# adaLN tiles of the FFNs in buffers of their own, requested two steps before they are reduced

## The chip, the cores and the metric

One core of a Trainium2 chip runs the whole program. The metric is the device time of one execution in microseconds, the median of several runs. The core has five engines that run side by side and meet only at semaphores: TensorE (PE), VectorE (DVE), ScalarE (ACT), GpSimd (POOL) and SyncE (SP). Here SP does nothing but request DMA transfers from HBM, in the order of its program; DVE, ACT and PE too work through their instructions strictly in order, so that one that waits holds up all that stand behind it on its engine.

## What is computed

Two layers, each of three sub-layers: FFN, token mixer, FFN. Every sub-layer is modulated by a conditioning vector c (adaLN) and followed by a residual sum and a LayerNorm:

```python
mod = (silu(c) @ ada_w[l] + ada_b[l]).reshape(-1, 3, 3, 1024)   # shift, scale, gate of three sub-layers
g, up = split(u @ w_in);   F(u) = (silu(g) * up) @ w_out        # FFN, D_FF = 2816
h = 0.5 * F(x * (1 + scale) + shift)
x = LayerNorm(ALPHA * x + (1 + gate) * h)
```

There are 256 tokens, so x fits on chip; what comes from HBM is the weights, each used once. The adaLN weights are part of them: each of the 18 vectors of 1024 numbers (shift, scale, gate of six sub-layers) is a 1024x1024 matrix times silu(c).

## The kernel before

**Products.** Every product of the network is done as three matmuls of numbers split in a high and a low part (`split_mm`, L286 to L288 with the weights stationary, L290 to L292 with the activations stationary): high by high, low by high, high by low. A weight tile of 128x1024 (512 KB) comes into a buffer named `raw` (L259), ACT casts its high part `hi` (L262), DVE subtracts to get the low part `lo` (L267), and then PE can use it.

**The buffers.** The tag `raw` has five such buffers. A request on SP waits until the buffer it will overwrite has been read for the last time, for a weight by the subtraction L267.

**The FFN.** There are 22 blocks f of 128 hidden columns. The first two of all but the first FFN are done for token half t = 0, then t = 1, with the tokens stationary (tiles `acc`, `th`, `h`; the transposes back to hidden columns, `hT`, are L609). From then on a block is one `hidden(f)`: 48 matmuls into a PSUM bank `mm`, tanh on ACT (`th`, L522), two DVE operations (`th` L523 and `h` L525, the last readers of the bank), a cast on ACT (`hh`, L531) and a subtraction on DVE (`hl`, L532). The down products (`acc<-hi,hh` and so on) follow a few blocks later. In PSUM the banks rotate, so PE cannot begin a block until the h of an earlier one has been made.

**The boundary.** At the end of a sub-layer `boundary` makes the residual sum and the statistics (L401 to L408) of token half 0 and then 1, normalises (L418), and PE transposes the result (L426), from which the next `uh` and `ul` are made (L432 to L437). The scale and shift of the LayerNorm are applied to x itself later (L485, L486). PE fills the time with down products and with the first blocks of the next FFN.

**adaLN.** The vectors of the next sub-layer and the gate of the current one are made beside this. `ada_cols` gives four steps to a vector; each step requests two tiles of 128x1024 on SP (L307) and reduces each of them on DVE (L308, multiply by silu(c) and sum along the row). An FFN has twelve such steps, 24 tiles, spread over the blocks f (the last one, with nothing behind it, four); a mixer has twelve. The 128 reductions of the program therefore use the same five `raw` buffers as the weights, and a step's request stands next to its reduction in the program.

**Order.** The order on each engine is fixed before the run, by a scheduler that takes instructions by priority and by modelled readiness. `behind()` keeps the first steps of a sub-layer from being placed before the boundary's main work.

**Other buffers.** The tag `big8` has three buffers of 8 KB a partition. It holds tiles of the mixers (`mh`, `ml`, `merged`, the live row tiles), the start's `xT` and `ada0`, and `rt` of each boundary. In an FFN's blocks they are not used until `rt` is (L629).

Of the kernel before, what the change touches and what calls it, by code (L numbers as in the profile page):

```python
# [11 lines left out]
F32 = mybir.dt.float32  # L12
# [44 lines left out]
RB, QB = 5, 15  # L57
# [6 lines left out]
GD = 3  # L64
# [39 lines left out]
SS = 1  # L104
PJ = 5
AFF = 3
AM = 42
ROW_M = 10

# [35 lines left out]
def trunk(ctx: ExitStack, tc: tile.TileContext, x, xT, crow, ada0, adac, adab, w_in0, w_in0x, gcol, bcol, ln_g, ln_b,  # L145
          w_in, w_out, mpair, mv0, mv12, mbrA, mbr, mwo, bgate, bforget, eye, rot, masks, out):
    nc = tc.nc
    P = 128
    cp = ctx.enter_context(tc.tile_pool(name="cp", bufs=1))
    wp = ctx.enter_context(tc.tile_pool(name="wp", bufs=3))  # L150
    ap_ = ctx.enter_context(tc.tile_pool(name="ap", bufs=2))
    sp = ctx.enter_context(tc.tile_pool(name="sp", bufs=2))
    mp = ctx.enter_context(tc.tile_pool(name="mp", bufs=1))
# [140 lines left out]

    mods = {(l, s): {} for l in range(DEPTH) for s in range(3)}

    def ada_cols(l, s, v):

        key = ("shift", "scale", "gate")[v]

        def run(c):
            if c == 0:
                mods[(l, s)][key] = ap_.tile([P, KT], F32, tag=key, bufs=2, name=key)
            t = mods[(l, s)][key]
            for n in (2 * c, 2 * c + 1):
                raw = wp.tile([P, 1024], F32, tag="raw", bufs=RB, name="raw")
                nc.sync.dma_start(raw, adac[l, s, v, n])  # L307
                nc.vector.tensor_tensor_reduce(raw, raw, cond_row, 0.5, adab_sb[:, l * 3 + s, v, n:n + 1],  # L308
                                               ALU.mult, ALU.add, accum_out=t[:, n:n + 1])

        return [lambda c=c: run(c) for c in range(4)]

    def ada_gate(l, s):

        def spread():
            ps = tp_bank()
            nc.tensor.transpose(ps[:KT, :P], mods[(l, s)]["gate"], ident)
            col = ap_.tile([KT, P], F32, tag="grow8", bufs=1, name="grow8")
            nc.scalar.copy(col, ps[:KT, :P])
            flat = dp.tile([KT, P], F32, tag="gflat", bufs=2, name="gflat")  # L320
            nc.gpsimd.dma_start(flat, col)
            G = ap_.tile([P, D], F32, tag="row", bufs=3, name="G")
            fetch_row(G, flat.rearrange("a b -> (a b)"))
            mods[(l, s)]["G"] = G

        return spread
# [18 lines left out]
    def fetch_row(dst, row):  # L345

        with tc.issue_after(held["pool"]):
            nc.gpsimd.memset(dst, 0.0)
        nc.gpsimd.dma_start(dst[0:P:32], row.partition_broadcast(4))

    def spread_row(dst):
        for h in range(SH):
            hs = slice(h * (D // SH), (h + 1) * (D // SH))
            with tc.issue_after(held["lo"]):
                nc.vector.stream_shuffle(dst[:, hs], dst[:, hs], [0] * 32)

    def both(*fs):
        def run():
            for f in fs:
                f()  # L360
        return run

    def sub_steps(l, s, nxt):

        st = mods[(l, s)]
        nx = ada_cols(*nxt, 0) + ada_cols(*nxt, 1) if nxt else [lambda: None for _ in range(8)]

        def fetch(key, row):
            st[key] = ap_.tile([P, D], F32, tag="row", bufs=3, name=key)
            fetch_row(st[key], row)  # L370

        before = {}
        for key, n, src in (("g", ROW_M if s == 1 else ROW_G, ln_g), ("b", ROW_M if s == 1 else ROW_B, ln_b)):
            before.setdefault(n, []).append(lambda key=key, src=src: fetch(key, src[l * 3 + s]))
            before.setdefault(n + GD, []).append(lambda key=key: spread_row(st[key]))
        before.setdefault(GG, []).append(lambda: ada_gate(l, s)())
        before.setdefault(GG + GD, []).append(lambda: spread_row(st["G"]))
        seq = ada_cols(l, s, 2) + nx + ([lambda: None] * (ROW_M + GD + 1 - 12) if s == 1 else [])
        return [both(*before.get(n, []), f) for n, f in enumerate(seq)]


# [112 lines left out]
    def ffn(l, s, u, nxt, steps, first=False):  # L494
# [12 lines left out]
        def hidden(f):  # L507
            k0 = N0 if f in part else 0
            w = load(w_in[fi, f, :, k0:].rearrange("p a b -> p (a b)"))
            ps = mm_bank()  # L510
            for g in range(2):
                for kt in range(k0, KT):
                    split_mm(ps[:, g * 256:(g + 1) * 256], w((kt - k0) * 256 + g * 128, 128),
                             uh[:, kt, :], ul[:, kt, :], kt == k0, kt == KT - 1)
            if f in part:
                nc.vector.tensor_tensor(part[f], part[f], ps, op=ALU.add)
                ps = part[f]
            post(f, ps[:, :256], ps[:, 256:])
# [93 lines left out]
        for f in range(f0, NF):  # L612
            hidden(f)
            if not first and f >= AFF and held["affine"]:
                held["affine"].pop(0)()
# [23 lines left out]
    def mixer(l, u, nxt, steps):  # L639
# [12 lines left out]
        def on(n, *fs):  # L652
            turns.setdefault(n, []).extend(fs)
# [323 lines left out]
        def plan():  # L977
# [27 lines left out]
            for n, piece in enumerate(held["affine"]):  # L1005
                on(AM + n, piece)

# [114 lines left out]
    for l in range(DEPTH):  # L1122
        u = ffn(l, 0, u, (l, 1), sub_steps(l, 0, (l, 1)), first=l == 0)
        u = mixer(l, u, (l, 2), sub_steps(l, 1, (l, 2)))
        nxt = (l + 1, 0) if l + 1 < DEPTH else None
        u = ffn(l, 2, u, nxt, sub_steps(l, 2, nxt))
# [55 lines left out]
```

## Time and profile before

| what | value |
|---|---|
| time, median of 3 runs | 1320.27 us (1318.94 to 1322.92) |
| the profiled execution's own time | 1320.82 us |
| its span on the engines | 1319.0 us |
| PE busy | 1271.0 us, 96% |
| DVE busy | 1036.8 us, 79% |
| ACT busy | 653.7 us, 50% |
| moved by SP's queue | 298 MB, 66.5% of the 16 DMA engines |

The sub-layers lie at about 0 to 205 us (FFN), 205 to 455 (mixer), 455 to 655 (FFN), 655 to 850 (FFN of the second layer), 850 to 1100 (mixer) and 1100 to 1319 (FFN). The table's shares are means over all of them. In the list of waits a row names the engine and tile that sat idle, what it waited for, and how long in total, how often and how long at most; in a timeline a row is one instruction or a run of equal ones, with the idle time before it in brackets. Start-to-start, matmuls of 256 columns follow one another at about 0.12 us and those of 512 at 0.23 us, though each shows a longer time of its own, since they overlap.

### The profile page before, as it was taken

Reading aid. Unit: us, or ns where it says so; the run is one execution under the profiler, and the core shown is the slowest. Engines: PE = TensorE matmul, PEld = TensorE weight load, DVE = VectorE, ACT = ScalarE, POOL = GpSimd, SP = SyncE. Lnnn points to the kernel's source line nnn. Section 1 sums busy time; section 2 is a strip of 40 time slices with the busy share of each in tenths; the row PEclk is TensorE's granted clock in tenths of the full one; section 3 lists DMA queues with packets and bytes.
Section 4 is the critical chain, followed back from the end, with each engine's and each line's share of the span. In section 5 each row is a group of like instructions: output and inputs, shape, how many; then the busy total and the mean of one; then the engine's idle time right before and its main releaser. Section 6 shows DMA issues by size and latency. Waiting matters only on the chain.

```text
span 1319.0 us, 23422 instructions
## 1 busy us (share of the span) xinstructions
PE 1271.0 (96%) x9178; PEld 1180.2 (89%) x9178; DVE 1036.8 (79%) x1701; ACT 653.7 (50%) x1023; POOL 134.2 (10%) x150
## 2 busy tenths in 40 slices
PE   6999999999999999999999999999999999999997
PEld 5989988899899889999989999898989998899995
DVE  7788888999765799876698877698976758976565
ACT  4555355456664454444355444445657544554440
POOL 0130000304111000000000000022050110000000
PEclk9999999999999999999999999999999999999999
DMA  9889893767665638987449887356676554595540
GB/s 340 327 290 330 294 306 133 243 191 245 228 216 180 215 128 312 309 279 262 159 166 320 289 296 237 115 178 219 217 235 233 192 192 160 208 317 193 185 137 32
DMA packets 85846, 300.41 MB, mean 228 GB/s; under 512 B 10604, under 2 KB 12316, under 8 KB 85736
## 3 DMA queue, kind: packets, MB, share of 16 engines
q1 hardware_dynamic: 84392, 298.00, 66.5%
q8 instruction: 72, 1.18, 0.4%
q10 hardware_dynamic: 576, 0.60, 0.1%
q0 software_dynamic: 768, 0.32, 0.1%
q14 instruction: 38, 0.31, 0.1%
HBM read 297.81 MB, written 1.07 MB: 227 GB/s over the span
## 4 chain that ended last, share of the span: by engine, by line
PE 41%; issue 26%; DVE 13%; DMA 12%; ACT 4%; POOL 3%; DVEq 0%; ACTq 0%; SPq 0%; POOLq 0%
PE mm L286 8%; PE mm L287 8%; PE mm L288 8%; DMA raw<-in_w_in_dram 7%; DVE lo L267 5%; PE acc L292 3%; PE acc L290 3%; PE acc L291 3%; ACT hi L262 2%; POOL lb L968 2%; DVE raw L308 2%; DMA raw<-in_adac_dram 1%; PE tp L286 1%; PE tp L287 1%; PE tp L288 1%
## 5 line engine op out<-in xcount | busy, mean ns | idle before, releaser
L267 DVE TENSOR_TENSOR lo<-raw,hi 128x1024 fp32r<-128x1024 f32 (+2 forms) x421 | 507.7, 1220 | 165.4 <-ACT hi L262 163.7
L262 ACT CAST hi<-raw 128x1024 fp32r<-128x1024 f32 (+1 forms) x422 | 434.0, 1040 | 331.2 <-PE mm L287 133.4
L286 PE MATMUL mm<-uh,hi 128*128 128x256 f32 x2032 | 576.0, 284 | 2.5 <-DVE h L525 2.5
L287 PE MATMUL mm<-ul,hi 128*128 128x256 f32 x2032 | 572.4, 282 | 0.0
L288 PE MATMUL mm<-uh,lo 128*128 128x256 f32 x2032 | 571.5, 282 | 0.0
L286 PEld LDWEIGHTS mm<-uh,hi 128*128 128x128 f32 x2032 | 384.6, 189 | 9.8 <-issue 5.4
L287 PEld LDWEIGHTS mm<-ul,hi 128*128 128x128 f32 x2032 | 384.8, 189 | 1.3
L288 PEld LDWEIGHTS mm<-uh,lo 128*128 128x128 f32 x2032 | 384.3, 189 | 0.3
L308 DVE CUSTOM_DVE_ANT_0 raw<-raw,cond_row,adab 128x1024 f32<-128x1024 f32 x128 | 164.9, 1300 | 37.7 <-DMA raw<-in_adac_dram 37.4
L290 PE MATMUL acc<-hi,hh 128*128 128x512 f32 x352 | 140.4, 399 | 1.8 <-ACT hh L531 1.8
L291 PE MATMUL acc<-lo,hh 128*128 128x512 f32 x352 | 139.0, 395 | 0.0
L292 PE MATMUL acc<-hi,hl 128*128 128x512 f32 x352 | 137.7, 396 | 1.2 <-DVE hl L532 1.2
L292 PEld LDWEIGHTS acc<-hi,hl 128*128 128x128 f32 x352 | 65.9, 187 | 18.4 <-DVE hl L532 2.0
L531 ACT CAST hh<-h 128x256 fp32r<-128x256 f32 x82 | 33.2, 405 | 99.0 <-DVE h L525 97.5
L290 PEld LDWEIGHTS acc<-hi,hh 128*128 128x128 f32 x352 | 66.1, 188 | 16.8 <-ACT hh L531 2.8
L291 PEld LDWEIGHTS acc<-lo,hh 128*128 128x128 f32 x352 | 66.1, 188 | 13.9
L408 POOL TENSOR_TENSOR rstd<-rstd,nhalf 128x1 f32<-128x1 f32 x12 | 7.6, 633 | 496.9 <-DVE rstd L407 496.9
L290 PE MATMUL acc<-hi,uh 128*128 128x256 f32 (+1 forms) x128 | 39.1, 305 | 2.2 <-ACT uh L436 2.1
L532 DVE TENSOR_TENSOR hl<-h,hh 128x256 fp32r<-128x256 f32 x74 | 31.1, 420 | 12.6 <-ACT hh L531 12.6
L522 ACT ACTIVATE th<-mm 128x256 f32<-128x256 f32 x74 | 27.9, 377 | 24.8 <-PE mm L288 24.7
L292 PE MATMUL acc<-hi,ul 128*128 128x256 f32 (+1 forms) x128 | 38.8, 303 | 0.0
L291 PE MATMUL acc<-lo,uh 128*128 128x256 f32 (+1 forms) x128 | 38.4, 300 | 0.0
(242 smaller groups left out, 1504.8 us busy)
## 6 DMA issues: line engine op xcount, KB each, us to landing
raw<-in_w_in_dram SPq DMA_DIRECT2D x174, 512.0 KB, 5.6
raw<-in_adac_dram SPq DMA_DIRECT2D x128, 512.0 KB, 5.2
raw<-in_mpair_dram SPq DMA_DIRECT2D x104, 512.0 KB, 5.2
raw<-in_w_out_dram SPq DMA_DIRECT2D x88, 512.0 KB, 5.2
ada<-in_ada_dram SPq DMA_DIRECT2D x16, 512.0 KB, 6.9
raw<-in_mwo_dram SPq DMA_DIRECT2D x16, 512.0 KB, 3.9
raw<-in_mv_dram SPq DMA_DIRECT2D x16, 384.0 KB, 3.8
raw<-in_mbr_dram SPq DMA_DIRECT2D x12, 512.0 KB, 3.8
```

The lines of the kernel that those rows point to most:

```text
L262: nc.scalar.copy(hi[:, :half], raw[:, :half])
L267: held["lo"] = nc.vector.tensor_sub(lo[:, :half], raw[:, :half], hi[:, :half].bitcast(F32)).ins
L286: nc.tensor.matmul(ps, lhsT=wh, rhs=xh, start=start, stop=False)
L287: nc.tensor.matmul(ps, lhsT=wh, rhs=xl, start=False, stop=False)
L288: nc.tensor.matmul(ps, lhsT=wl, rhs=xh, start=False, stop=stop)
L290: nc.tensor.matmul(ps, lhsT=xh, rhs=wh, start=start, stop=False)
L291: nc.tensor.matmul(ps, lhsT=xh, rhs=wl, start=False, stop=False)
L292: return nc.tensor.matmul(ps, lhsT=xl, rhs=wh, start=False, stop=stop).ins
L308: nc.vector.tensor_tensor_reduce(raw, raw, cond_row, 0.5, adab_sb[:, l * 3 + s, v, n:n + 1], ALU.mult, ALU.add, accum_out=t[:, n:n + 1])
L522: nc.scalar.activation(th, pg, AF.Tanh, scale=0.5)
L531: nc.scalar.copy(hh, h)
L532: eng.tensor_sub(hl, h, hh.bitcast(F32))
```

## The change

In the four FFNs a step's two tiles are the halves of one tile `adac` of 128x2x1024 from the tag `big8`, three buffers. The request is split from the reduction: `ahead` requests the first three pairs at the first step (two, and the one that is two further on), and then at each step the pair two further on. The mixers keep `raw` and request at the step itself. The weights of an FFN have the five `raw` buffers to themselves. Bytes, matmuls, casts, subtractions and reductions are the same in number.

```diff
+AHEAD = 2
-    def ada_cols(l, s, v):
+    def ada_cols(l, s, v, own):
+        got = {}
+        def fetch(c):
+            if own:
+                two = mp.tile([P, 2, 1024], F32, tag="big8", bufs=3, name="adac")
+                got[c] = [two[:, 0], two[:, 1]]
+            else:
+                got[c] = [wp.tile([P, 1024], F32, tag="raw", bufs=RB, name="raw") for _ in range(2)]
+            for h in range(2):
+                nc.sync.dma_start(got[c][h], adac[l, s, v, 2 * c + h])
-        def run(c):
+        def reduce(c):
...
-            for n in (2 * c, 2 * c + 1):
-                raw = wp.tile([P, 1024], F32, tag="raw", bufs=RB, name="raw")
-                nc.sync.dma_start(raw, adac[l, s, v, n])
+            for h, raw in enumerate(got.pop(c)):
+                n = 2 * c + h
                 nc.vector.tensor_tensor_reduce(raw, raw, cond_row, 0.5, adab_sb[:, l * 3 + s, v, n:n + 1],
                                                ALU.mult, ALU.add, accum_out=t[:, n:n + 1])
-        return [lambda c=c: run(c) for c in range(4)]
+        return [(lambda c=c: fetch(c), lambda c=c: reduce(c)) for c in range(4)]
+    def ahead(pairs, n):
+        def step(i):
+            if i == 0:
+                for f, _ in pairs[:n]:
+                    f()
+            if i + n < len(pairs):
+                pairs[i + n][0]()
+            pairs[i][1]()
+        return [lambda i=i: step(i) for i in range(len(pairs))]
...
-        nx = ada_cols(*nxt, 0) + ada_cols(*nxt, 1) if nxt else [lambda: None for _ in range(8)]
+        own = s != 1
+        pairs = ada_cols(l, s, 2, own) + (ada_cols(*nxt, 0, own) + ada_cols(*nxt, 1, own) if nxt else [])
+        work = ahead(pairs, AHEAD if own else 0) + ([] if nxt else [lambda: None for _ in range(8)])
...
-        seq = ada_cols(l, s, 2) + nx + ([lambda: None] * (ROW_M + GD + 1 - 12) if s == 1 else [])
+        seq = work + ([lambda: None] * (ROW_M + GD + 1 - 12) if s == 1 else [])
```

What the scheduler makes of it is seen at three places. Lines of the changed kernel are up to 23 higher (L318 is the reduction L308, L424 is L401, L508 is L485, L268 is L267), and the numbers behind the names are counted anew.

**Place 1, the requests of SP at the start of the second layer's first FFN (655 us).** Before:

```order
L259 DMA raw_7823<-in_w_in_dram 128x1024
L259 DMA raw_7829<-in_w_in_dram 128x1024
L307 DMA raw_7896<-in_adac_dram 128x1024
L307 DMA raw_7899<-in_adac_dram 128x1024
L259 DMA raw_7902<-in_w_in_dram 128x1024
L259 DMA raw_7908<-in_w_in_dram 128x1024
```

After; adac_7871 and adac_7874 are the first two pairs of the gate, x2 is a pair's two requests, and raw_7799 and raw_7805 answer to raw_7823 and raw_7829:

```order
L260 DMA raw_7799<-in_w_in_dram 128x1024
L310 DMA adac_7871<-in_adac_dram 128x1024 x2
L310 DMA adac_7874<-in_adac_dram 128x1024 x2
L310 DMA adac_7877<-in_adac_dram 128x1024 x2
L310 DMA adac_7955<-in_adac_dram 128x1024 x2
L260 DMA raw_7805<-in_w_in_dram 128x1024
L260 DMA raw_7883<-in_w_in_dram 128x1024
```

Eight ada requests now stand between the first and the second half of one weight block; the other FFNs have eight in a row too (the first) or six (the other two).

**The same place on DVE, the boundary's chain for token half 1.** Its residual sum (`rt`, x1), statistics (`st6`, `mvar`, `rstd`) and xhat, before:

```order
L403 BN_STATS st6_7466<-x1_109 128x6
L486 TENSOR_TENSOR x0_108<-x0_108,b_6200 128x512
L406 BN_AGGR mvar_7468<-st6_7466 128x2
L407 TENSOR_SCALAR rstd_7470<-mvar_7468 128x1
L418 TENSOR_SCALAR x1_109<-x1_109,mvar_7468,rstd_7470 128x256 x4
```

After:

```order
L426 BN_STATS st6_7442<-x1_109 128x6
L508 TENSOR_TENSOR x0_108<-x0_108,g_6112 128x512
L429 BN_AGGR mvar_7444<-st6_7442 128x2
L318 ISA adac_7874,gate_7880<-adac_7874,cond_row_84,adab_89 128x1024
L318 ISA gate_7880 128x1
L430 TENSOR_SCALAR rstd_7446<-mvar_7444 128x1
L509 TENSOR_TENSOR x0_108<-x0_108,b_6190 128x512
L441 TENSOR_SCALAR x1_109<-x1_109,mvar_7444,rstd_7446 128x256 x4
```

A reduction has moved between the aggregate and rstd, and the last of the four affine operations on x0 has moved behind rstd. The first reduction of the same pair stands earlier in the same chain:

```order
L424 TENSOR_TENSOR rt_7333<-acc_5622,G_6199 128x512
L318 ISA adac_7874,gate_7880<-adac_7874,cond_row_84,adab_89 128x1024
L318 ISA gate_7880 128x1
L425 SCALAR_TENSOR_TENSOR x1_109<-x1_109,rt_7333 128x512
L508 TENSOR_TENSOR x0_108<-x0_108,g_6112 128x512
```

Before, nothing stood between this rt and the sum on x1; no reduction of this FFN stood ahead of the second token half's xhat.

**Place 2, DVE in the first blocks behind that boundary.** h of the first token half (L607 before, L630 after), before:

```order
L607 SCALAR_TENSOR_TENSOR h_7645<-th_7642,acc_7551 128x256
L485 TENSOR_TENSOR x1_109<-x1_109,g_6121 128x512
L267 TENSOR_TENSOR lo_7716<-raw_7713,hi_7715 128x1024
L267 TENSOR_TENSOR lo_7722<-raw_7719,hi_7721 128x1024
L267 TENSOR_TENSOR lo_7790<-raw_7787,hi_7789 128x1024
L267 TENSOR_TENSOR lo_7796<-raw_7793,hi_7795 128x1024
L267 TENSOR_TENSOR lo_7826<-raw_7823,hi_7825 128x1024
L267 TENSOR_TENSOR lo_7832<-raw_7829,hi_7831 128x1024
```

After:

```order
L318 ISA adac_7871,gate_7880<-adac_7871,cond_row_84,adab_89 128x1024
L318 ISA gate_7880 128x1
L268 TENSOR_TENSOR lo_7692<-raw_7689,hi_7691 128x1024
L268 TENSOR_TENSOR lo_7698<-raw_7695,hi_7697 128x1024
L268 TENSOR_TENSOR lo_7766<-raw_7763,hi_7765 128x1024
L268 TENSOR_TENSOR lo_7772<-raw_7769,hi_7771 128x1024
L268 TENSOR_TENSOR lo_7802<-raw_7799,hi_7801 128x1024
L268 TENSOR_TENSOR lo_7808<-raw_7805,hi_7807 128x1024
L630 SCALAR_TENSOR_TENSOR h_7621<-th_7618,acc_7527 128x256
```

h has moved behind six subtractions, and a reduction has come in ahead of them; on PE the transposes of this h (hT) stand 63 matmuls later than before. Twelve DVE rows further on, after:

```order
L268 TENSOR_TENSOR lo_8082<-raw_8079,hi_8081 128x1024
L268 TENSOR_TENSOR lo_8148<-raw_8145,hi_8147 128x1024
L546 SCALAR_TENSOR_TENSOR th_7750<-th_7750,mm_7701 128x256
L268 TENSOR_TENSOR lo_8076<-raw_8073,hi_8075 128x1024
L548 SCALAR_TENSOR_TENSOR h_7753<-th_7750,mm_7701 128x256
```

Of the corresponding block before (h_7777 of mm_7725) this stands there:

```order
L523 SCALAR_TENSOR_TENSOR th_7774<-th_7774,mm_7725 128x256
L308 ISA raw_7974,gate_7895<-raw_7974,cond_row_84,adab_89 128x1024
L308 ISA gate_7895 128x1
L525 SCALAR_TENSOR_TENSOR h_7777<-th_7774,mm_7725 128x256
L308 ISA raw_7977,gate_7895<-raw_7977,cond_row_84,adab_89 128x1024
```

A subtraction has taken the reduction's place between th and h. The buffer of hi_8075 is the one whose last reader on PE is the last down product of the pair of blocks 0 and 1 (`acc<-hi_7771,hl_7686`); right behind that product PE has the first matmul into mm_7895, which uses the bank of mm_7701 and so waits for h_7753.

**Place 3, DVE at the end of the first FFN (190 us): the last block's th and h.** Before:

```order
L267 TENSOR_TENSOR lo_2327<-raw_2324,hi_2326 128x768
L523 SCALAR_TENSOR_TENSOR th_2126<-th_2126,mm_2077 128x256
L267 TENSOR_TENSOR lo_2333<-raw_2330,hi_2332 128x768
L525 SCALAR_TENSOR_TENSOR h_2129<-th_2126,mm_2077 128x256
L267 TENSOR_TENSOR lo_2339<-raw_2336,hi_2338 128x768
L532 TENSOR_TENSOR hl_2132<-h_2129,hh_2131 128x256
```

After:

```order
L318 ISA adac_1834,scale_1725<-adac_1834,cond_row_84,adab_89 128x1024
L318 ISA scale_1725 128x1
L268 TENSOR_TENSOR lo_2321<-raw_2318,hi_2320 128x768
L318 ISA adac_1834,scale_1725<-adac_1834,cond_row_84,adab_89 128x1024
L318 ISA scale_1725 128x1
L268 TENSOR_TENSOR lo_2315<-raw_2312,hi_2314 128x768
L409 TENSOR_TENSOR gd_2240<-gcol_102,scale_1725 128x8
L410 TENSOR_TENSOR bd_2241<-bcol_103,scale_1725 128x8
L546 SCALAR_TENSOR_TENSOR th_2114<-th_2114,mm_2065 128x256
L411 TENSOR_TENSOR bd_2241<-bd_2241,shift_1455 128x8
L548 SCALAR_TENSOR_TENSOR h_2117<-th_2114,mm_2065 128x256
```

The subtraction between th and h is gone, and the last two reductions of the FFN, which stood far earlier, have come in ahead of th. PE's own order is the same as before everywhere but at the starts of the three later FFNs, where hT and the first down products come later; the mixers are the same on PE.

## Rows read from the trace of the kernel before

**Rows 1.** The page's first part: busy time, share and instructions of each engine.

```profile
PE 1271.0 (96%) x9178; PEld 1180.2 (89%) x9178; DVE 1036.8 (79%) x1701; ACT 653.7 (50%) x1023; POOL 134.2 (10%) x150
```

**Rows 2.** Waits of PE: tile, what it waited for, total us, times, longest.

```profile
PE mm L426 <- DVE x L418: 5.2, 5, 1.7
...
PE mm L286 <- DVE h L525: 2.5, 3, 1.0
...
PE acc L290 <- ACT hh L531: 1.8, 1, 1.8
PE hT L609 <- DVE h L607: 1.2, 3, 0.6
PE acc L292 <- DVE hl L532: 1.2, 1, 1.2
```

**Rows 3.** Waits of DVE, the row of the ada reductions.

```profile
DVE raw L308 <- DMA raw<-in_adac_dram: 37.4, 26, 3.9
```

**Rows 4.** The page's costliest groups: busy us, mean ns of one | idle before.

```profile
L308 DVE CUSTOM_DVE_ANT_0 raw<-raw,cond_row,adab 128x1024 f32<-128x1024 f32 x128 | 164.9, 1300 | 37.7 <-DMA raw<-in_adac_dram 37.4
```

**Rows 5.** Windows: length, busy us by engine, clock, DMA share, GB/s.

```profile
490.00:560.00 70.00, 69.41 (x488) 64.59 (x488) 62.68 (x93) 34.86 (x47) 3.66 (x5) 1.00 0.91 314
...
655.00:680.00 25.00, 24.00 (x173) 21.95 (x172) 22.59 (x46) 13.93 (x28) 2.69 (x4) 1.00 0.16 51
```

**Rows 6.** Timeline of DVE late in the second FFN: start us, us, instruction, [idle before].

```profile
599.56 1.28 DVE L308 CUSTOM_DVE_ANT_0 raw<-raw,cond_row,adab 128x1024 f32<-128x1024 f32 x1 [3.92 <-DMA raw<-in_adac_dram]
...
603.37 1.28 DVE L308 CUSTOM_DVE_ANT_0 raw<-raw,cond_row,adab 128x1024 f32<-128x1024 f32 x1
...
604.58 0.41 DVE L525 SCALAR_TENSOR_TENSOR h<-th,mm 128x256 f32<-128x256 f32 x1
```

**Rows 7.** Timeline of PE, the rows in which it had waited, from six stretches.

```profile
170.38 0.36 PE L286 MATMUL mm<-uh,hi 128*128 128x256 f32 x1 [0.82 <-DVE h L525]
...
195.13 0.50 PE L290 MATMUL acc<-hi,hh 128*128 128x512 f32 x1 [1.77 <-ACT hh L531]
...
605.05 0.39 PE L286 MATMUL mm<-uh,hi 128*128 128x256 f32 x1 [0.71 <-DVE h L525]
...
668.64 0.44 PE L426 MATMUL mm<-ident,x 128*128 128x128 f32 x2 [0.92 <-DVE x L418]
...
797.58 0.39 PE L286 MATMUL mm<-uh,hi 128*128 128x256 f32 x1 [0.96 <-DVE h L525]
...
1145.50 0.73 PE L292 MATMUL acc<-hi,hl 128*128 128x512 f32 x2 [1.16 <-DVE hl L532]
```

**Rows 8.** Timeline of DVE from 666 us: the boundary at Place 1, then Place 2.

```profile
666.50 0.68 DVE L486 TENSOR_TENSOR x<-x,b 128x512 f32<-128x512 f32 x1
667.09 0.20 DVE L406 BATCH_NORM_AGGREGATE mvar<-st 128x2 f32<-128x12 f32 x1
667.33 0.15 DVE L407 TENSOR_SCALAR rstd<-mvar 128x1 f32<-128x1 f32 x1
668.17 1.38 DVE L418 TENSOR_SCALAR x<-x,mvar,rstd 128x256 f32<-128x256 f32 x4 [0.69 <-POOL rstd L408]
...
673.65 5.76 DVE L267 TENSOR_TENSOR lo<-raw,hi 128x1024 fp32r<-128x1024 f32 x5
```

**Rows 9.** Timeline of SP's queue at Place 1: start, how long the pair took to issue.

```profile
650.16 25.06 SPq L259 DMA_DIRECT2D raw<-in_w_in_dram  x2
```

**Rows 10.** Timelines of ACT and DVE in the first blocks at Place 2.

```profile
679.04 1.05 ACT L262 CAST hi<-raw 128x1024 fp32r<-128x1024 f32 x1 [1.77 <-DMA raw<-in_w_in_dram]
...
694.45 1.22 DVE L267 TENSOR_TENSOR lo<-raw,hi 128x1024 fp32r<-128x1024 f32 x1 [0.20 <-ACT hi L262]
```

**Rows 11.** Timeline of DVE at Place 3, between the last th and h.

```profile
192.97 0.41 DVE L523 SCALAR_TENSOR_TENSOR th<-th,mm 128x256 f32<-128x256 f32 x1
193.30 0.95 DVE L267 TENSOR_TENSOR lo<-raw,hi 128x768 fp32r<-128x768 f32 x1
194.16 0.41 DVE L525 SCALAR_TENSOR_TENSOR h<-th,mm 128x256 f32<-128x256 f32 x1
```

## The prediction

> **What bounds the kernel now.** The first view is the page's busy times: PE works in 1271.0 of 1319.0 us and nothing else comes near it [rows 1]. So the change, which takes no matmul away, can only fill holes in PE, and the second view, PE's list of waits, says how large they are. In the blocks of the FFNs PE stood still behind h (L525) for 2.5 us in three places, behind hh for 1.8, behind h of the first two blocks (L607) for 1.2 and behind hl for 1.2 [rows 2]: 6.7 us in all, half a per cent. At the boundaries it waited 5.2 us more for the normalised x (L418). That is the most that better-fed FFNs can return. The third view is DVE's list of waits: 37.4 us in 26 places in which a reduction stood at DVE's head and its tile had not come [rows 3]. This is what the change goes for, and the reader is to see that 37.4 us there are 6.7 at most on PE: DVE catches up between.
>
> How one becomes the other is seen in the timelines. At 599.56 a reduction starts after 3.92 us of waiting for its tile; two subtractions, th and another reduction follow; h starts at 604.58 [rows 6] and PE, which wants its bank, gets going 0.71 us late at 605.05. The same shape costs 0.82 us at 170.38 and 0.96 at 797.58, and at 1145.50 PE waits 1.16 us for an hl that stands behind a late weight [rows 7].
>
> **What the change removes.** With tiles requested two steps early, a reduction finds its data, if there is room in time for the transfers. There is: from 655 to 680 us the DMA engines are 16% busy while SP sits 25.06 us on a pair of weight requests whose buffers aren't free [rows 5, 9], and ada pairs with buffers of their own can come in ahead of them. In mid-FFN there is less: 91% busy at 314 GB/s [rows 5]. The waits behind late tiles should go: 2.5 + 1.2 = 3.7 us of [rows 2]. The bounds are 0 (h still stands behind reductions, which at 1.30 us each [rows 4] are in DVE's order as before) and 3.7; I take 3.7, since at three of the four places the wait begins with a late transfer.
>
> The 1.8 us for hh at Place 3 may go either way. The subtraction between th and h took 0.95 us there [rows 11] and is gone; the one ahead of th is now a reduction or two. If their tiles have landed and DVE is early, PE gains up to 1.3 of the 1.77 us [rows 7]; if DVE comes to them late, two reductions cost 1.2 us more. I take nothing, with +1.2 and -1.3 as ends. The waits for L607 in the third and sixth sub-layer stay: the order of those steps is nearly the same.
>
> **What it adds, at Place 1.** Token half 1 of the boundary into the fourth sub-layer is a chain on DVE without a hole down to rstd at 667.33, and PE was already standing there: its transposes of x start at 668.64 after 0.92 us of waiting [rows 7, 8]. Into this chain two reductions have been placed. One costs 1.21 us start to start (603.37 to 604.58 [rows 6]); one affine operation of about 0.6 us (666.50 to 667.09 [rows 8]) moves behind rstd, into the 0.69 us in which DVE waits for POOL anyway. So 2 x 1.21 - 0.6 = +1.8 us, and nothing covers it. It is less only if PE's first-half work lasts longer, and the order gives PE nothing more to do; more if adac_7874 has not landed. It is requested directly behind the first of the two weights at 650.16, two pairs at under 1 us a request, and wanted at about 659.5, so it will have. Bounds 0.6 (one reduction hidden after all) and 3.0; I take 1.8.
>
> **At Place 2, first step.** h of token half 0 now waits behind six subtractions, the last of which wants the second half of a weight, raw_7805. Its buffer comes free with lo_7692, the first of the six: that started at 673.65 [rows 8], and now at 673.65 + 1.8 (boundary) + 1.21 (a reduction more) - 0.94 (h and an affine operation moved away) = 675.7, done at 676.9. In the kernel before, the same request went out when SP came free at 650.16 + 25.06 = 675.2 [rows 9] and its cast began at 679.04 [rows 10], 3.8 us later. So the cast begins at about 680.8 to 681.1, takes 1.05, the subtraction 1.22, and h 0.41: hT at about 683.8. On PE the transposes stood at about 673.6 and now have 63 more matmuls of 256 columns ahead of them, some 7.4 us at 0.117 each, so that PE, 1.8 us later at the boundary, gets there at about 682.8. A new wait of about 1.0 to 1.1, against 0.4 to 0.5 that was lost there before: +0.8 us as I put it, with bounds of 0 (h is fed in time) and 1.6.
>
> **At Place 2, second step.** Behind the last down product of blocks 0 and 1 PE goes to mm_7895, which wants h_7753, which stands on DVE behind lo_8076, whose cast on ACT waits for that very down product, since it frees the buffer. The chain runs with PE idle from end to end: 1.05 (cast, [rows 10]) + 1.22 (subtraction, [rows 10]) + 0.41 (h, [rows 6]) = 2.7 us. No timing of the engines avoids it, since each link is an order in the program or a buffer. In the kernel before, nothing of the kind stood between th_7774 and h_7777, only a reduction. I take 2.7; the bounds are 2.4 (overlaps of neighbours on DVE, whose starts are about 0.08 us closer than their lengths) and 3.2 with semaphores between.
>
> I walked the starts of the second and the sixth FFN sub-layer for the same pattern and found none: there the reductions are placed behind x1's last `ul`.
>
> **The sum.** -3.7 + 0 + 1.8 + 0.8 + 2.7 = +1.6 us on 1320.8 us of the profiled execution, 1322.4. That execution lies 0.5 us above the median, so 1321.9 in terms of the median: +0.1%. A measurement of this kernel tells about 0.3% (4 us) from no change; the forecast is that it shows none.
>
> **A rule weighed against the rows.** At Place 1 DMA share is 16% before, and eight requests for ada are now ahead of raw_7805 in SP's order [rows 5]. The last of them, adac_7955, waits for the second reduction inside the boundary chain, ends at about 669, and lands by 675, two us before raw_7805 is requested; then it costs nothing. The Trainium skill ("DMA: Bandwidth & Descriptors", section "Queues, rings and completion order") says that on each DMA engine the descriptors of SP's queue are consumed in ring order, so a weight requested behind ada tiles that are still on their way would wait for them. No row before shows the two in this order. By that rule, if the boundary slips, raw_7805 would lie behind two tiles of 512 KB. In the kernel's own rows two such tiles take 1.05 MB / 314 GB/s = 3.3 us [rows 5], and PE would stand that much longer before hT: 1321.9 + 3.3 = 1325.2.
>
> **The rivals.**
> - *Reductions in time, but still in the way: slower.* DVE works strictly in order, and early tiles don't shorten the reductions of an FFN. If the waits behind h are due to these standing before th and h (at 604.58 h comes directly after one [rows 6], and at Place 3 two now stand ahead of th), then the 3.7 us don't come back and Place 3 costs its 1.2: 1320.8 + 5.3 + 1.2 = 1327.3, 1326.8 by the median. It decides as soon as less than about 1.4 of the 3.7 us come back with all else as summed (1324.2 is the 0.3% line). For it: DVE is busy 62.7 of 70 us in mid-FFN [rows 5]. Against it: three of those waits start with a transfer.
> - *The three costs aren't there: faster.* If ACT and DVE run far enough ahead that Places 1 and 2 lose nothing and the gains come with Place 3 and L607 on top, 1320.8 - 3.7 - 1.3 - 1.2 = 1314.6, 1314.1 by the median. Against it: PE is already waiting at Place 1, and the chain at Place 2 is closed.
> - *It doesn't matter to PE.* The tiles arrive early, DVE's 37.4 us vanish, and PE, fed by other buffers, gains and loses under 1 us: 1320.3. For it: 37.4 us of DVE make at most 3.7 on PE as it is.
> - *The ring order above*: 1325.2.
>
> **How the numbers follow.** The sum as worked out 0.45 (its own range, with its terms' bounds, about 1319 to 1325); it doesn't matter 0.12; faster 0.12; still in the way 0.27; ring order 0.04. Same: 0.45 + 0.12 = 0.57; slower: 0.27 + 0.04 = 0.31; faster: 0.12. The range leaves about a tenth on each side: 1316.0 to 1327.0.
>
> **What would show it.** In the profile after: DVE's wait for ada tiles falls from 37.4 us to a few in the mixers; PE's wait for h in the blocks falls at 170, 605 and 798 us; the transposes of x at Place 1 start about 1.8 us later, with a wait near 2.7 us; hT of the first half waits about 1 us; and about 15 us after that a new wait of PE for h of some 2.7 us stands in the list, alone as large as all waits for h before. If that last row is missing, the second step at Place 2 is wrong; if the waits for h at 605 and 798 remain, the gain is. A new wait of PE on weights (`lo` or `hi`) anywhere in an FFN would mean that ada transfers pushed weights back, which I have priced at only one place.

## The result, and the profile after

The changed kernel takes 1332.12 us, the median of 4 runs (1330.92 to 1335.83), against 1320.76 us of before beside it: a ratio of 1.0083, with a 95% interval of 1.0059 to 1.0107. It is 11 us slower. The forecast was +0.1%, within 0.3%, and the range ended at 1327; both are wrong.

The profiled execution took 1333.07 us, with a span of 1331.3 where it was 1319.0. The page's first part, as in [rows 1]:

```profile
PE 1275.6 (96%) x9178; PEld 1181.3 (89%) x9178; DVE 1036.3 (78%) x1701; ACT 652.8 (49%) x1023; POOL 137.1 (10%) x150
```

Work is the same on all engines, so the 12.3 us are waits and slower stretches of PE: for the same instructions PE is busy 4.6 us longer (the clock, last section) and idle 7.7 us longer. Its list of waits after (tile, what it waited for, us in total, times, longest), to be held against [rows 2]; the lines have moved up by 23 (L449 is L426, L548 is L525, L555 is L532, L630 is L607):

```profile
PE mm L449 <- DVE x L441: 6.1, 5, 1.8
PE acc L293 <- DVE hl L555: 4.6, 6, 1.7
PE hT L632 <- DVE h L630: 4.2, 3, 2.1
...
PE mm L287 <- DVE h L548: 2.6, 1, 2.6
```

The 1.8 us for hh are gone, and of the three waits for h in the blocks none is left; the 2.6 are one new wait. But hl has gone from 1.2 to 4.6, and hT from 1.2 to 4.2. One step of PE comes once in each boundary, the transposes of the second token half's x (L449, before L426), and so shows how the time runs away. PE's timeline before, from the five stretches (start us, us, instruction, idle before in brackets):

```profile
213.55 0.44 PE L426 MATMUL mm<-ident,x 128*128 128x128 f32 x2 [1.61 <-DVE x L418]
...
475.95 0.44 PE L426 MATMUL mm<-ident,x 128*128 128x128 f32 x2 [0.55 <-DVE x L418]
...
861.03 0.44 PE L426 MATMUL mm<-ident,x 128*128 128x128 f32 x2 [1.69 <-DVE x L418]
...
1124.70 0.44 PE L426 MATMUL mm<-ident,x 128*128 128x128 f32 x2 [0.48 <-DVE x L418]
```

and after:

```profile
209.48 0.44 PE L449 MATMUL mm<-ident,x 128*128 128x128 f32 x2 [1.70 <-DVE x L441]
...
476.79 0.44 PE L449 MATMUL mm<-ident,x 128*128 128x128 f32 x2 [0.50 <-DVE x L441]
...
674.75 0.44 PE L449 MATMUL mm<-ident,x 128*128 128x128 f32 x2 [1.77 <-DVE x L441]
...
873.97 0.44 PE L449 MATMUL mm<-ident,x 128*128 128x128 f32 x2 [1.69 <-DVE x L441]
...
1136.13 0.44 PE L449 MATMUL mm<-ident,x 128*128 128x128 f32 x2 [0.49 <-DVE x L441]
```

Differences, with 668.64 of [rows 7]: -4.1, +0.8, +6.1, +12.9, +11.4, and +12.3 at the end of the span. So the first FFN gained 4.1 us. The first mixer, on which the change does nothing, lost 4.9; the second FFN with its boundary lost 5.3 and the third 6.8; the second mixer gave 1.5 back. The mixers' part is mostly TensorE's clock, which fell to half for short stretches worth about 1.7 us each (last section): in the first mixer three times after and once before, in the second once after and twice before, in the third FFN once after and not before. Without these the first mixer lost about 1.5 us, the second nothing, and the second and third FFN 5.3 and 5.1.

What stopped PE in the later FFNs (PE's timeline after, from six stretches):

```profile
493.40 0.44 PE L632 MATMUL hT<-ident,h 128*128 128x128 f32 x2 [2.07 <-DVE h L630]
...
566.73 0.50 PE L293 MATMUL acc<-hi,hl 128*128 128x512 f32 x1 [1.50 <-DVE hl L555]
...
705.74 0.39 PE L287 MATMUL mm<-uh,hi 128*128 128x256 f32 x1 [2.63 <-DVE h L548]
...
768.58 0.50 PE L293 MATMUL acc<-hi,hl 128*128 128x512 f32 x1 [1.73 <-DVE hl L555]
...
1152.34 0.44 PE L632 MATMUL hT<-ident,h 128*128 128x128 f32 x2 [1.68 <-DVE h L630]
```

The two for hT stood before at:

```profile
490.62 0.44 PE L609 MATMUL hT<-ident,h 128*128 128x128 f32 x2 [0.59 <-DVE h L607]
...
1138.99 0.44 PE L609 MATMUL hT<-ident,h 128*128 128x128 f32 x2 [0.23 <-DVE h L607]
```

Place 2's wait at 705.74 is the chain of the prediction, 2.63 us against 2.7. DVE's timeline after, around it, shows the links: h stands behind the subtraction that came in:

```profile
703.80 0.41 DVE L546 SCALAR_TENSOR_TENSOR th<-th,mm 128x256 f32<-128x256 f32 x1
704.13 1.22 DVE L268 TENSOR_TENSOR lo<-raw,hi 128x1024 fp32r<-128x1024 f32 x1
705.27 0.41 DVE L548 SCALAR_TENSOR_TENSOR h<-th,mm 128x256 f32<-128x256 f32 x1
```

The other four have weight subtractions ahead of h or hl too, and the prediction doesn't have them. At 493.40 a subtraction that itself waits 1.24 us for its cast stands between th and h:

```profile
490.13 0.42 DVE L628 SCALAR_TENSOR_TENSOR th<-th,acc 128x256 f32<-128x256 f32 x1
491.79 1.23 DVE L268 TENSOR_TENSOR lo<-raw,hi 128x1024 fp32r<-128x1024 f32 x1 [1.24 <-ACT hi L263]
492.93 0.41 DVE L630 SCALAR_TENSOR_TENSOR h<-th,acc 128x256 f32<-128x256 f32 x1
```

That cast on ACT had waited for the transfer of its weight:

```profile
490.71 1.05 ACT L263 CAST hi<-raw 128x1024 fp32r<-128x1024 f32 x1 [1.75 <-DMA raw<-in_w_in_dram]
```

And before 566.73, a reduction waits 3.11 us for its tile, and then two subtractions, th, h, the spreading of two rows (L376) and another subtraction stand ahead of hl:

```profile
558.54 1.28 DVE L318 CUSTOM_DVE_ANT_0 adac<-adac,cond_row,adab 128x1024 f32<-128x1024 f32 x1 [3.11 <-DMA adac<-in_adac_dram]
...
559.75 2.36 DVE L268 TENSOR_TENSOR lo<-raw,hi 128x1024 fp32r<-128x1024 f32 x2
...
565.12 1.22 DVE L268 TENSOR_TENSOR lo<-raw,hi 128x1024 fp32r<-128x1024 f32 x1
566.25 0.42 DVE L555 TENSOR_TENSOR hl<-h,hh 128x256 fp32r<-128x256 f32 x1
```

So the tiles still come late in the later FFNs. DVE's waits for ada tiles, after, for the whole span (raw are the mixers', adac the FFNs'):

```profile
DVE raw L318 <- DMA raw<-in_adac_dram: 21.7, 18, 3.7
DVE adac L318 <- DMA adac<-in_adac_dram: 13.9, 8, 3.1
```

The same view before, mixers only (205 to 455 and 855 to 1100 us), and then the second and third FFN (455 to 655 and 655 to 855); in the first and the last it has no such row:

```profile
DVE raw L308 <- DMA raw<-in_adac_dram: 10.4, 9, 3.1
...
DVE raw L308 <- DMA raw<-in_adac_dram: 11.6, 9, 3.5
...
DVE raw L308 <- DMA raw<-in_adac_dram: 9.1, 4, 3.9
...
DVE raw L308 <- DMA raw<-in_adac_dram: 6.4, 4, 2.8
```

Of the 37.4 us of [rows 3], 22.0 stood in the mixers, which the change leaves alone. The FFNs had 15.5 and now have 13.9, of which 2.9 stand in the first. In the program a tile is asked for two steps ahead, but on SP's queue it stands behind weight requests that wait for buffers: the request after which the reduction of 558.54 could start went out at 551.95, and its data landed 6.6 us later.

```profile
551.95 0.42 SPq L310 DMA_DIRECT2D adac<-in_adac_dram  x1
```

### The profile page after: what moved, and what is told of

Same layout as the page of the kernel before. It is cut to its first block, busy times and chain, and to the rows that moved or that the text cites. A ratio compares the mean times of both kernels' runs of the same rounds, so it can differ in the third digit from the quotient of the medians.

```text
span 1331.3 us, 23410 instructions
## 1 busy us (share of the span) xinstructions
PE 1275.6 (96%) x9178; PEld 1181.3 (89%) x9178; DVE 1036.3 (78%) x1701; ACT 652.8 (49%) x1023; POOL 137.1 (10%) x150
## 3 DMA queue, kind: packets, MB, share of 16 engines
HBM read 297.81 MB, written 1.07 MB: 225 GB/s over the span
## 4 chain that ended last, share of the span: by engine, by line
PE 46%; issue 26%; DVE 12%; DMA 8%; ACT 4%; POOL 3%; DVEq 0%; SPq 0%; POOLq 0%; ACTq 0%
PE mm L287 9%; PE mm L288 9%; PE mm L289 9%; DVE lo L268 4%; PE acc L293 4%; PE acc L291 4%; PE acc L292 4%; DMA raw<-in_adac_dram 3%; DMA raw<-in_w_in_dram 2%; ACT hi L263 2%; POOL lb L991 2%; PE tp L287 1%; PE tp L288 1%; PE tp L289 1%; DMA gflat<-grow 1%
## 5 line engine op out<-in xcount | busy, mean ns | idle before, releaser
L268 DVE TENSOR_TENSOR lo<-raw,hi 128x1024 fp32r<-128x1024 f32 (+2 forms) x421 | 507.9, 1223 | 175.8 <-ACT hi L263 174.9
L318 DVE CUSTOM_DVE_ANT_0 adac<-adac,cond_row,adab 128x1024 f32<-128x1024 f32 x80 | 102.0, 1282 | 14.1 <-DMA adac<-in_adac_dram 13.9
L318 DVE CUSTOM_DVE_ANT_0 raw<-raw,cond_row,adab 128x1024 f32<-128x1024 f32 x48 | 63.3, 1325 | 21.9 <-DMA raw<-in_adac_dram 21.7
L291 PEld LDWEIGHTS acc<-hi,hh 128*128 128x128 f32 x352 | 66.1, 188 | 15.5 <-ACT hh L554 1.6
L555 DVE TENSOR_TENSOR hl<-h,hh 128x256 fp32r<-128x256 f32 x74 | 31.3, 423 | 14.1 <-ACT hh L554 14.1
```

What stands on the lines that cost most here:

```text
L268: held["lo"] = nc.vector.tensor_sub(lo[:, :half], raw[:, :half], hi[:, :half].bitcast(F32)).ins
L291: nc.tensor.matmul(ps, lhsT=xh, rhs=wh, start=start, stop=False)
L555: eng.tensor_sub(hl, h, hh.bitcast(F32))
```

## The experiments

Three theories were set against each other. Theory 1: the loss is made by order; in the later FFNs DVE has reductions and weight subtractions ahead of the operations for which PE waits. Theory 2: the loss has little to do with the later FFNs, but with the mixer behind the first and TensorE's clock. Theory 3: the early transfers push the weights back. All ratios are to the kernel before, run beside, with their 95% intervals, and are taken over the runs, so that they are not exactly the quotient of two medians. The median of before varied from 1320.8 to 1323.5 us between the sets of runs, so ratios are compared and not times.

**The first FFN alone.** Own buffers and early requests there, the rest as before:

```diff
-        own = s != 1
+        own = s == 0 and l == 0
```

> Only the first FFN has own buffers and early requests; the other three are as in the kernel before. Compared with before (1320.8), the changed kernel was 4.1 us ahead at the end of the first FFN and lost it all later. Theory 1 (the loss is made at the starts and in the blocks of the later FFNs, by what stands before h and hl on DVE): the 4.1 us stay, 1316 to 1318 us. Theory 2 (the lead is lost anyway behind the FFN, in the mixer and to the TensorE clock, whatever the later FFNs do): 1320 to 1322 us.

Measured: 1317.04 us, 0.9968 (0.9944 to 0.9991), 0.32% or 4.2 us faster. The gain of the first FFN stays; theory 2 falls in so far as nothing takes it back by necessity. PE's only wait for h in the blocks is then one in the second FFN, where the kernel before had one too (605.05, [rows 7]):

```profile
PE mm L287 <- DVE h L548: 1.1, 1, 1.1
```

**The other three FFNs alone.**

```diff
-        own = s != 1
+        own = s != 1 and (l, s) != (0, 0)
```

> The change in the three later FFNs only; the first is as before. The parts should add: 1.0083 (whole change) minus 0.9968 (first FFN alone) gives about 1.0115 of before, 1334 to 1338 us. If the first FFN's lead had been given back by some coupling, it would be at 1.008.

Measured: 1338.73 us, 1.0126 (1.0084 to 1.0169). The parts add: 0.9968 and 1.0126 make 1.0094, and the whole is 1.0083. The change is two changes, one worth -0.3% and one that costs +1.2%.

**Own buffers, but requested at their own step**, in all FFNs, and then in the first alone:

```diff
-AHEAD = 2
+AHEAD = 0
```

> The changed kernel with own buffers, but each pair requested at its own step. The order at Places 1 and 2 is the same as in the changed kernel. Theory 1: the loss stays, and the reductions wait for their tiles again: 1331 to 1336 us. Theory 3 (the early requests do the harm): 1320 to 1325 us.

> Own buffers in the first FFN alone, each pair requested at its own step. With requests two steps ahead it was 0.9968 of before. With own buffers and no early request in all FFNs the first FFN ended 2.2 us later than in the kernel before. If the early request makes the gain: 1.000 to 1.003. If the buffers do: 0.996 to 0.998.

Measured: 1.0115 (1.0077 to 1.0153) and 1.0011 (0.9990 to 1.0032). The early request doesn't do the harm: without it the kernel is slower by at least as much, and theory 3 falls. Nor were the weights late as a whole: ACT's waits for the transfers of the FFNs' first weights, over the whole span, before and after:

```profile
ACT hi L262 <- DMA raw<-in_w_in_dram: 91.4, 76, 5.8
...
ACT hi L263 <- DMA raw<-in_w_in_dram: 30.2, 24, 2.8
```

The early request makes the gain: in the first FFN the buffers alone bring nothing, with early requests 0.9968. In the profile of the second the waits for h have stayed as in [rows 2], and the one for hh has become one for hl:

```profile
PE mm L287 <- DVE h L548: 2.5, 3, 1.4
...
PE acc L293 <- DVE hl L555: 1.1, 1, 1.1
```

**Steps kept behind the boundary.** The changed kernel; the first four steps of the later FFNs may not be placed ahead of the boundary's work, so that the two reductions of Place 1 and the chain of Place 2 are gone from the order:

```diff
-                with behind() if held["left"] > 0 else ExitStack():
+                with behind() if held["left"] > 0 or (not first and ran < 4) else ExitStack():
```

> The changed kernel with one edit: in the three later FFNs the first four steps, not only those near the boundary by count of loads, are kept behind the boundary's main work on DVE. The order then has no reduction in the boundary chain of Place 1, and neither the six subtractions ahead of h nor the subtraction between th and h at Place 2. Theory 1 (order at Places 1 and 2 costs what the trace of the changed kernel shows there: about 1.8 at the transposes of x, 2.6 at the first matmul behind h, and a clock drop between): 1332.1 - 4.5 to 6 = 1326 to 1327.5 us. Theory 3 (early transfers as such push weights back all over the FFNs): stays at 1330 to 1332 us.

Measured: 1327.60 us, 1.0057 (1.0037 to 1.0078): 0.26 points below the change, about 3.4 us, where 4.5 to 6 were expected; the two intervals overlap, so that this gain is not told from none. The wait at 705.74 is gone, but the waits for hl and hT are not (4.8 and 3.7 us), and in the third FFN they have grown; PE's timeline there:

```profile
760.63 0.80 PE L293 MATMUL acc<-hi,hl 128*128 128x512 f32 x1 [2.67 <-DVE hl L555]
```

**h and hl first.** The changed kernel; what PE waits for in the blocks (th, h, hh, hl) gets a higher priority in the scheduler than the loading of weights, whose subtractions were ahead of it:

```diff
-            post(f, ps[:, :256], ps[:, 256:])
+            with tc.high_priority(offset=HP + 20):
+                post(f, ps[:, :256], ps[:, 256:])
```

> The changed kernel with one edit: th, h, hh and hl of the blocks have a higher priority in the scheduler than the loading of weights. The subtraction between th and h at Place 2 is gone, the two reductions in the boundary chain at Place 1 stay. Theory 1: the 2.6 us wait for h at 705 us and the waits for hl at 567 and 769 us (1.7 each) go: 1332.1 - 4 to 6 = 1326 to 1328 us. If only the boundary mattered: 1331 to 1333 us.

Measured: 1323.53 us, 1.0016 (0.9997 to 1.0036). This edit alone takes 0.67 points of the loss (about 8.8 us, where 4 to 6 were expected), with the two reductions of Place 1 in place. PE's waits then:

```profile
PE hT L633 <- DVE h L631: 5.2, 3, 2.4
...
PE acc L293 <- DVE hl L556: 0.9, 3, 0.4
...
PE mm L287 <- DVE h L549: 0.2, 1, 0.2
```

What is left is hT, whose h (first two blocks) this edit doesn't reach.

**The same priority in the kernel before**, as a control, and with the change in the first FFN only:

> The kernel before with that priority alone. If it mends only what the change had done to the order (weights run further ahead once they have all five buffers): no difference, 0.999 to 1.001. If it is a gain of its own: 0.995 to 0.998, and then the 0.0067 that it gave the changed kernel says less about the change.

> Own buffers and early requests in the first FFN alone, and th, h, hh, hl of the blocks ahead of the loading of weights. Alone, the first gave 0.9968 of before. If that priority helps the blocks of the later FFNs also without the change there, 0.993 to 0.996; if it only mends what the change had done to the order, 0.996 to 0.998.

Measured: 0.9990 (0.9966 to 1.0014) and 0.9962 (0.9940 to 0.9984). Without the change in the later FFNs the priority does nothing that can be told from none. So it is no gain of its own: it mends the order that the change had made.

**Both edits, and then the priority for the first two blocks too** (their th, h and hT, and the splits of hT, inside the same `high_priority`; one line per statement, not shown):

> The changed kernel with both edits at once: the first four steps of the later FFNs kept behind the boundary, and th, h, hh, hl of the blocks ahead of the loading of weights in the scheduler's priority. If the two costs are separate (the boundary, about 4 us with its clock drop, and what stands ahead of h and hl in the blocks, about 8), both go: 0.9985 of before or less, 1318 to 1321 us where before is 1322. If they are largely the same stalls seen twice (the forced chain behind the boundary is removed by either edit), the sum is no better than the second edit alone: 1.0016 of before.

> The changed kernel with the first four steps kept behind the boundary, and the raised priority for th, h, hh, hl and hT of the first two blocks as well as of the later ones. With gating and the priority of the later blocks alone, 7.5 us of PE's waits were for that h of the first two blocks. If what DVE puts ahead of h is the whole cost of the change in the later FFNs, these waits fall to about 2 and the time to 0.996 to 0.999 of before, near that of the change in the first FFN alone (0.9968). If it stays at 1.002 or above, early requests in the later FFNs cost something else.

> As the kernel that came to 0.999 of before, but without keeping the steps behind the boundary: the two reductions are back in the boundary chain of Place 1, and h, hl and hT keep their raised priority everywhere. The difference between the two is the price of those two reductions. As predicted it is 1.8 us (1.0004); with a clock drop behind the longer wait 3.5 us, 1.0015 to 1.002. If it isn't slower than 0.999, the boundary term was no cost by itself.

Measured: both edits 1.0038 (1.0016 to 1.0060), neither of the two outcomes expected, and no better than the priority alone (1.0016); with the first two blocks as well 0.9990 (0.9970 to 1.0009); the same without keeping the steps back 0.9987 (0.9961 to 1.0012). With both edits PE waited 7.5 us for h of the first two blocks:

```profile
PE hT L633 <- DVE h L631: 7.5, 3, 3.1
```

and with these raised as well there is no row for it left; of the blocks only this remains:

```profile
PE acc L293 <- DVE hl L556: 2.7, 6, 0.9
```

So giving these operations priority undoes the loss of the change, from 1.0083 to 0.9987. That it acts through what DVE does ahead of h, hl and hT is read from PE's waits; the same edits also raise the tanh and the cast of h on ACT and the transposes on PE, which were not tried apart. Two ends stay open. What is left to 0.9968 of the first FFN alone is within the intervals, so some of the later FFNs' loss may remain. And the priority of the first two blocks was not tried in the kernel before; PE waited 1.2 us for hT there [rows 2], so it has little to gain.

The reductions inside the boundary chain cost nothing that the total shows: 0.9987 with them, 0.9990 without. At their place PE does wait longer, 1.83 us for x and 0.85 for a ul, against 1.50 for x; PE's timelines with the reductions:

```profile
660.99 0.38 PE L293 MATMUL acc<-hi,ul 128*128 128x256 f32 x1 [0.85 <-DVE ul L460]
...
668.45 0.62 PE L449 MATMUL mm<-ident,x 128*128 128x128 f32 x2 [1.83 <-DVE x L441]
```

and without them:

```profile
666.99 0.44 PE L449 MATMUL mm<-ident,x 128*128 128x128 f32 x2 [1.50 <-DVE x L441]
```

That is about 1.2 us, under what these runs can tell. The two kernels differ in more than that: keeping the steps back makes PE wait longer for x at the other two starts, 1.07 us each against 0.55, which hides about as much.

**Four buffers for the weights.** The changed kernel with `RB = 4`:

> The changed kernel with four instead of five buffers for weights. If the harm in the blocks comes from weights running further ahead (their subtractions stand before h and hl because five buffers are now theirs alone), four buffers undo part of it: the wait for h at 705 us goes, 1.002 to 1.006 of before. If weights are short of time instead, PE gets new waits for lo and hi and the time rises above 1.010.

Measured: 1349.57 us, 1.0225 (1.0183 to 1.0267): the opposite of the first expectation. PE's waits of mm for h come to 1.1 us in all, as that had it, but PE got waits in nearly all stages, the mixers among them, which also have only four then. So it doesn't tell whether five buffers of their own let the weights run too far ahead; it shows that four are too few for this kernel. Which of the two makes the scheduler put the subtractions first, the free buffers or the absence of ada requests between the weights' on SP, is not settled. Own buffers without early requests have the same order at Places 1 and 2 and the same loss, so it comes with the buffers.

No combination was clearly better than the change in the first FFN alone, 0.9968, or with the priority, 0.9962; both beat both kernels.

## Why the prediction was wrong

- **The bound on the gain** (6.7 us on PE at most) was passed by no run (the best, 0.9962, gained about 5 us), and the waits it named went: at 170, 195, 605 and 798 us PE no longer waits. The gain in the first FFN, 4.1 us, was larger than the 0.8 I had given it. About 0.65 of it stands at 23 us already, and the kernel before with the priority alone had such a lead there too, so it isn't the change's. The rest is the wait at 170 and the term for hh at Place 3, which came out beyond its good end of 1.3 (the whole wait of 1.77 went): th at 188.44 is followed by h at 188.89 with no subtraction between, and the two reductions ahead of them had their data.

```profile
188.44 0.42 DVE L546 SCALAR_TENSOR_TENSOR th<-th,mm 128x256 f32<-128x256 f32 x1
...
188.89 0.42 DVE L548 SCALAR_TENSOR_TENSOR h<-th,mm 128x256 f32<-128x256 f32 x1
```

- **The two costs that were worked out** came nearly as put on DVE, but only one of them on PE. The chain at Place 2: 2.63 against 2.7. The boundary: from rt to xhat DVE took 668.17 - 658.86 = 9.3 us before and 674.28 - 663.12 = 11.2 after, +1.85 against 1.8:

```profile
658.86 0.68 DVE L401 TENSOR_TENSOR rt<-acc,G 128x512 f32<-128x512 f32 x1
...
663.12 0.68 DVE L424 TENSOR_TENSOR rt<-acc,G 128x512 f32<-128x512 f32 x1
...
674.28 1.38 DVE L441 TENSOR_SCALAR x<-x,mvar,rstd 128x256 f32<-128x256 f32 x4 [0.46 <-POOL rstd L431]
```

PE's wait for x, however, went from 0.92 to 1.77 only, not to the 2.7 that were to show it: about half of the term reached PE, so "nothing covers it" was wrong. The first step of Place 2 (+0.8) didn't come: h of the first half was there at 688.07 and PE came to hT at 688.78, with no wait. About 1.7 us of PE's delay was the half clock at 677, so by this estimate the term was hidden by luck and not refuted. Removing both places from the order brought 0.26 points, not the 0.4 of the sum; other waits grew in their place.

- **The step that failed** is "The waits for L607 in the third and sixth sub-layer stay", together with the sentence that found no such pattern at those starts and priced weights at only one place. These waits went from 0.59 to 2.07 us at 493 and from 0.23 to 1.68 at 1152, and waits for hl of 1.5 and 1.7 us came up in mid-FFN. In PE's list hT grew by 3.0 us where the sum had nothing, and hl by 3.4 (1.2 to 4.6) where it had a gain of 1.2. I looked for a closed chain between two of PE's instructions, found one, and left out what has none: every subtraction that moves ahead of th, h or hl puts its 1.2 us before them and, if its weight hasn't landed, the wait for that too. At 493 DVE was not short of time; it stood idle for 1.24 us behind such a weight, with h behind it in its order. Before, a reduction with its tile there stood in that place. In mid-FFN it came on top of late ada tiles (3.11 us before 558.54). "DVE catches up between" was true of the old order and was carried over to the new one.

- **What 37.4 us were** was misread: 22.0 of them stand in the mixers. A split by stage would have shown that the change could touch 15.5, in eight places, none of them in the first FFN; so "the same shape" didn't hold at 170. Where the gain there comes from isn't fully shown. Weights come earlier in the first FFN (ACT's waits for them fell from 36.6 to 15.8 us up to 205 us), but they do so as well with own buffers and no early request (15.0), which gained nothing; there DVE waits 6.8 us for ada tiles, with early requests 2.9. So the early request is needed; early requests without own buffers were not run.

- **The rival that came nearest** is that reductions are still in the way, 1326.8; what stood in the way were mostly the weights' subtractions. The ring-order rival didn't occur and its rule was not put to the test: the last of the eight ada requests went out at 673.6 and landed within 4.7 us, the weight behind them went out at 681.16 and its cast began at 685.43, 4.3 us later, against 3.8 before.

- **The range.** The bounds of the terms add to -2.0 and +9.0 us, 1318.3 to 1329.3 by the median, not to "about 1319 to 1325"; the measured 1332.1 lies outside both.

- **The clock was not priced** (below): two more stretches at half clock, about 3.4 of the 12.3 us between the profiles.

## What to carry to other kernels

A total of waits on an engine that isn't the bound says little; split it by stage before working out what a change can reach, and then ask what the buffers that it frees will be filled with. Giving one stream its own buffers lets the other stream run ahead, and here the scheduler put the work for that stream ahead of the work that the bottleneck waits for, on an engine that works in order. So after such a change look at the order again, and at priorities. Try a change in each stage apart: here one stage gained 0.3% and three lost 1.2%.

## What the runs showed of the hardware

TensorE's granted clock fell to half (1.2 of 2.4 GHz) for short stretches right behind waits of PE. In the profile after there are five of them (from about 244, 339, 455, 677 and 875 us), in the profile before three (340, 863 and 989), beside one at the very end in both. Two windows on one of them after (length, busy us by engine, then the granted clock, DMA share, GB/s):

```profile
677.50:680.50 3.00, 3.00 (x15) 3.00 (x15) 3.00 (x7) 3.00 (x5) 0.00 (x0) 0.50 0.01 5
...
677.00:683.00 6.00, 6.00 (x38) 5.84 (x38) 6.00 (x11) 5.68 (x9) 0.00 (x0) 0.72 0.18 60
```

A mean of 0.72 over 6 us is 1.7 us of full clock lost, as much as a wait. The stretch at 455 comes behind a wait of 1.96 us for mh, and this one behind the 1.77 us for x at 674.75. Waits of 2.07 us at 493.40, 2.63 at 705.74 and 1.73 at 768.58 had no such stretch behind them, so a wait of that size does not decide it. Over all runs the mean granted clock was 0.9938 for the kernel before (31 runs), 0.9905 for the changed one (4 runs), 0.9902 with own buffers and no early request (6 runs), 0.9945 and 0.9933 for the two kernels whose waits for h and hT were gone (12 runs each) and 0.9942 for the change in the first FFN alone (12 runs). Between before and after, 0.0033 of 1325 us are 4.4 us of the 11, by this estimate. The slowest kernels here have the lowest clock; that PE's waits are the cause was not tried by itself.
